# The gate's last two column blocks as a group of seven products, and a tile of the third normed block moved to another pool

## The chip, the cores and the metric

One core of a Trainium2 chip runs the whole program as one launch. The metric is the time of an execution on the device in microseconds, as the median of several runs. TensorE does the matrix products, VectorE and ScalarE the elementwise work, GpSimd (POOL) and SyncE (SP) mainly issue transfers.

## The reference

A decoder block on 256 tokens of width 2048, in float32: a half-step SwiGLU feed-forward, a mixer (gated DeltaNet and stick-breaking attention) between one input and one output projection, a second half-step feed-forward, then a gated embedding and a last norm. Only the end is touched by the change:

```python
h = h + 0.5 * swiglu(rms_norm(h, ffn2_norm), ffn2_w_gu, ffn2_w_down)
gate = jax.nn.sigmoid(rms_norm(h, ple_norm) @ ple_w_gate)   # 2048 x 2048
h = h + gate * (p @ ple_w_proj)                              # p: 256 x 256
return rms_norm(h, final_norm)
```

## The kernel before

**Products in three passes.** Each float32 operand is split into a high part (a cast to fp32r, on ScalarE) and a low part (the rest, on VectorE), and a product is three matmuls: high x high, high x low, low x high. Columns of weights come in blocks of 512, the contraction in steps of 256 ("pairs" of 128). A pair of weights is one transfer of 512 KB into `raw` (4 buffers), a cast `whi` and a subtraction `wlo` (`weight_pair`, 3 buffers each), and 12 matmuls: 2 halves of the pair x 2 tiles of 128 tokens x 3 passes.

**Groups of seven products.** A `Group` takes two column blocks and both token tiles, and does the first `ns` pairs of the contraction by a scheme of seven products for eight (`product`, `halved`, `all_sums`): each product is one token tile, 3 x `ns` matmuls, on sums of quarters of the weights (`R`, four tiles) and sums of the left sides (`Sh`, `Sl`, made by `halves`). The four results are in four PSUM banks `c11, c21, c12, c22`. ScalarE copies a first product from one bank to another (L349), or copies `c21` to `part` (L352) for VectorE to subtract (L354). Two of the sums of quarters are done by VectorE (L309), two by a transfer that accumulates, issued on POOL (L316). What is left of the contraction are plain pairs that add to the same banks. A group's seven products run between the plain pairs of the group before it.

**The order.** `plan` writes a list `order` of weight loads for the whole kernel; `next_weights` walks it and keeps two pairs and one sum split ahead of use. Side work (norms, transposes, left sides) is in generators, in four `Lanes`, each advanced one step after every plain pair. The program is written in this order and a scheduler fixes each engine's instruction order from it; the keyword `keep_in_program_order` pins a few.

**The end of the kernel.** The last group of the second feed-forward is the down projection of columns 1024 to 2047. Between its plain pairs run the products of "behind", the group of the gate's blocks 0 and 1 with `NS_BEHIND = 2`. `norm_block` prepares the normed, transposed, split `nT` per block of 512 columns of h. Blocks 0 to 2 go by VectorE transposes of 32 x 32 (`tb`), a store to DRAM on SP and four loads back into one tile `tT`, in the pool "ffn", then four scalings each on ScalarE (L162) and VectorE (L163). The last block goes by TensorE transposes. Block 2's seven steps reach into the plain pairs of "behind". Then the pool "ffn" ends and the pool "fin" begins, in the same memory: `fg` (the last norm's gain, 1 MB), `ph`/`pl` (p, split), `hf` (h times that gain, 2 x 2048 columns).

In "fin": the 12 plain pairs of "behind", sorted by twos over its two blocks; after each block's last pair the embedding product `embed` (one pair of `w_pp`, 12 matmuls) and `gated` (sigmoid on ScalarE, two operations on VectorE, `sumsq` on ScalarE, the product with `fg` on VectorE). Block 2 follows with 8 plain pairs for both token tiles. For block 3 all 8 weight pairs stay in memory; token tile 0 is one column range of 512, token tile 1 two of 256, so that its last `gated` is short. After each token tile come `rstd`, four scalings and four stores of the output.

Of the kernel before, what the change touches and what calls it, by code (L numbers as in the profile page):

```python
# [10 lines left out]
F32 = mybir.dt.float32  # L11
F32R = mybir.dt.float32r
AF = mybir.ActivationFunctionType
# [3 lines left out]
P = 128  # L17
# [12 lines left out]
NS = 4  # L30
# [7 lines left out]
W_IN_ORDER = (2, 0, 4, 3, 1, 5, 8, 10, 12, 9, 11, 13, 6, 7)  # L38

NS_BEHIND = 2  # L40

PLAIN = {"1": 2, "2": 1}
EPS = 1e-6
# [4 lines left out]
def block_kernel(ctx, tc, a, out):  # L48
# [69 lines left out]
    def products(ps_t, t, xs, ws, n):  # L118

        for g, (whi, wlo) in enumerate(ws):  # L120
            for j in range(2):
                k = 2 * g + j
                xh, xl = xs(k)
                c = slice(t * P, (t + 1) * P)
                nc.tensor.matmul(ps_t, xh[:, c], whi[:, j, n], start=k == 0, stop=False)
                nc.tensor.matmul(ps_t, xh[:, c], wlo[:, j, n], start=False, stop=False)
                nc.tensor.matmul(ps_t, xl[:, c], whi[:, j, n], start=False, stop=k == 2 * len(ws) - 1)
# [100 lines left out]
    def block(j):  # L228
        return slice(j * NB, (j + 1) * NB)
# [19 lines left out]
    class Group:  # L249
# [8 lines left out]
        def __init__(self, kind, part, src, quarters, ns, bank, nb=0):  # L258
            self.kind, self.part, self.src, self.ns, self.nb, self.bank = kind, part, src, ns, nb, bank
            self.quarters, self.raw, self.first = quarters, {}, False  # L260
            self.seven = SEVEN_DOWN if kind == "dn" and part and nb == 0 else SEVEN
# [94 lines left out]
    def plan(n):  # L356
# [22 lines left out]
        if n == "2":  # L379
            src = [sources("w_behind", b) for b in range(2)]  # L380
            groups.append(Group("behind", len(PARTS), [x[0] for x in src], [x[1] for x in src], NS_BEHIND,
                                len(groups) % 2))
        if n == "1":

            groups[0].plain.sort(key=lambda x: x[1])
        made, carried = [], []
        for i, group in enumerate(groups):
            group.follower = follower = groups[i + 1] if i + 1 < len(groups) else None
            after = groups[i + 2] if i + 2 < len(groups) else None
            n_plain = len(group.plain)  # L390
            at, loads, carried = [], {0: carried}, []
            if follower is not None and follower.ns:
                first = 8 if not group.ns else 4 if follower.kind == "behind" else \
                    1 if group.kind == follower.kind or group.part and follower.kind == "dn" else 2
                at = [min(first + j, n_plain - 1) for j in range(7)]
                if not group.ns:
                    follower.first = n

                    loads.setdefault(max(at[0] - 5, 0), []).extend(follower.loads())
                if after is not None and after.ns:  # L400
# [5 lines left out]
            for j, (b, g) in enumerate(group.plain):  # L406
                todo.append(("plain", (b, g)))
                order.append(("pair", group.src[b][g]))
                if group.kind == "behind" and g == KD // 2 - 1:
                    order.append(("pair", a["w_pp"][b]))  # L410
                for x in range(7):
                    if at and at[x] == j:
# [10 lines left out]
    order += [("pair", a["w_pg"][2][g]) for g in range(KD // 2)] + [("pair", a["w_pp"][2])]  # L423
    order.append(("pair", a["w_pp"][3]))

    def left_sides(kind, his, los):

# [51 lines left out]
    def ffn(n, nT, r, scale, next_norm, stat):  # L479
        xs = picker(*nT)  # L480
        late = callable(r)
        with tc.tile_pool(name="ffn", bufs=1) as fp:
# [71 lines left out]
            for group, todo in ffn_plan[n]:  # L554
# [17 lines left out]
                for kind, one in todo:  # L572
# [28 lines left out]
                    if dn:  # L601
# [89 lines left out]


    with tc.tile_pool(name="fin", bufs=1) as fp:
        fg = fp.tile([P, D], F32, tag="fg", name="fg")
        nc.scalar.dma_start(out=fg, in_=a["final_norm"].broadcast_to([P, D]))
        ph = fp.tile([P, 2, T], F32R, tag="ph", name="ph")
# [9 lines left out]

        lanes.add(2, split_p())
        stat = new_stat()
        hf = fp.tile([P, 2, D], F32, tag="hf", name="hf")
        xs = picker(*nT)  # L710

        def gated(e, gt, c, t, col):
# [4 lines left out]
            nc.vector.tensor_tensor(out=s, in0=e, in1=s, op=ALU.mult)  # L717
            nc.vector.tensor_tensor(out=h[:, t, c], in0=h[:, t, c], in1=s, op=ALU.add)
# [9 lines left out]
        group, todo = ffn_plan["2"][-1]  # L728
        for _, (nb, g) in todo:
            whi, wlo = next_weights()  # L730
            for j in range(2):
                k = 2 * g + j
                xh, xl = xs(k)
                for t in range(2):
                    c = slice(t * P, (t + 1) * P)
                    gt, sp = group.banks[2 * nb + t], k == KD - 1
                    nc.tensor.matmul(gt, xh[:, c], whi[:, j, :], start=False, stop=False, skip_group_check=True)
                    nc.tensor.matmul(gt, xh[:, c], wlo[:, j, :], start=False, stop=False, skip_group_check=True)
                    nc.tensor.matmul(gt, xl[:, c], whi[:, j, :], start=False, stop=sp, skip_group_check=True)
            lanes.step()  # L740
            if g == KD // 2 - 1:
                e = embed(mm_ps)
                for t in range(2):
                    gated(e[t], group.banks[2 * nb + t], block(nb), t, nb)
        gt = [mm_ps("gt") for _ in range(2)]
        accumulate(gt, xs, KD)
        e = embed(mx_ps)
        for t in range(2):
            gated(e[t], gt[t], block(2), t, 2)

        e = embed(mx_ps)
        ws = [weight_pair(a["w_pg"][3][g], fp, KD // 2) for g in range(KD // 2)]
        for t in range(2):
            n = NB >> t
            for i in range(NB // n):
                gt = mm_ps("gt")[:, 0:n]
                products(gt, t, xs, ws, slice(i * n, (i + 1) * n))
                gated(e[t][:, i * n:(i + 1) * n], gt, slice(3 * NB + i * n, 3 * NB + (i + 1) * n), t, 3 + i)
            rt = rstd(stat, t)
            for j in range(4):  # L760
                c = slice(j * NB, (j + 1) * NB)

                if j == 0:
                    nc.scalar.activation(hf[:, t, c], hf[:, t, c], AF.Copy, scale=rt)
                else:
                    nc.vector.tensor_scalar(out=hf[:, t, c], in0=hf[:, t, c], scalar1=rt, scalar2=None, op0=ALU.mult)
                queue = nc.sync if j % 2 else nc.scalar
                queue.dma_start(out=out[t * P:(t + 1) * P, c], in_=hf[:, t, c])


class Later:
# [621 lines left out]
def _layout(i):  # L1393
# [28 lines left out]
    m["w_pg"] = _blocks(f["ple_w_gate"][0])  # L1422
# [20 lines left out]
```

## Time and profile before

| | |
|---|---|
| median of 3 runs | 1943.84 us (1942.93 to 1944.59) |
| the profiled execution | 1942.55 us, of which the span from first to last instruction is 1940.5 us |
| busy, share of the span | TensorE 99%, weight load 82%, VectorE 81%, ScalarE 60%, POOL 8% |
| moved by DMA | 477.14 MB, mean 246 GB/s |
| granted TensorE clock | 0.999 |

A profile row has the line of the program, the engine, the operation, `out<-in` with the program's tile names, the shape, a count, the busy time and the mean of one. In a timeline row the first two numbers are the start and the duration in us, and a bracket names the idle time before it and what ended it. A row of a wait is: who waited, for whom, us in total, times, longest. A row by window has the window, its length, then busy us and count of TensorE, weight load, VectorE, ScalarE and POOL, the granted clock, the DMA's share and GB/s. An engine name with q (SPq, ACTq) is that engine's queue issuing a transfer.

### The profile page before, as it was taken

How to read it: one execution, taken by the hardware profiler on the slowest of the kernel's cores; microseconds unless marked ns; L12 is line 12 of the kernel's file. 1: busy time of each engine (PE TensorE's matmuls, PEld its weight loads, DVE VectorE, ACT ScalarE, POOL GpSimd, SP SyncE). 2: the span in 40 equal slices, each digit the busy share in tenths (PEclk: the TensorE clock that was granted, in tenths of full speed). 3: DMA queues.
4: the chain of work that ended last, by engine and by line, in shares of the span. 5: the costliest groups of instructions: out<-in, count | busy, mean ns of one | idle time of the engine just before them, and what ended most of it. 6: DMA issues, size and time to landing. Idle time of an engine off the chain costs nothing.

```text
span 1940.5 us, 24108 instructions
## 1 busy us (share of the span) xinstructions
PE 1925.3 (99%) x8872; PEld 1591.1 (82%) x8872; DVE 1580.8 (81%) x1701; ACT 1169.9 (60%) x1356; POOL 148.7 (8%) x226
## 2 busy tenths in 40 slices
PE   9999999999999999999999999999999999999998
PEld 7888888888888888878788888888888888888887
DVE  7879878998789766797856679899889998888865
ACT  6656666666666557664555456566556665666654
POOL 0011110001001000010100000010000100001000
PEclk9999999999999999999999999999999999999999
DMA  8778888888988665556564776788888988889764
GB/s 309 268 237 283 251 290 284 275 274 248 286 274 263 215 220 172 176 168 213 166 209 157 244 280 233 227 282 289 247 270 289 295 261 263 267 263 291 231 214 148
DMA packets 143029, 477.14 MB, mean 246 GB/s; under 512 B 19520, under 2 KB 47168, under 8 KB 125632
## 3 DMA queue, kind: packets, MB, share of 16 engines
q1 hardware_dynamic: 106048, 297.97, 43.8%
q0 software_dynamic: 25920, 166.74, 31.1%
q10 hardware_dynamic: 10944, 10.91, 1.8%
q8 instruction: 69, 1.13, 0.2%
q14 instruction: 48, 0.39, 0.1%
HBM read 453.53 MB, written 22.02 MB: 245 GB/s over the span
## 4 chain that ended last, share of the span: by engine, by line
PE 93%; DVE 4%; DMA 1%; issue 1%; ACT 0%; POOL 0%; SPq 0%; POOLq 0%; DVEq 0%; ACTq 0%
PE d L594 5%; PE d L596 5%; PE d L595 5%; PE u L595 5%; PE u L596 5%; PE u L594 5%; PE g L345 5%; PE g L346 5%; PE g L344 5%; PE g L595 4%; PE g L596 4%; PE pj L113 4%; PE pj L114 4%; PE pj L115 4%; PE g L594 4%; PE d L344 3%
## 5 line engine op out<-in xcount | busy, mean ns | idle before, releaser
L78 ACT CAST whi<-raw 128x1024 fp32r<-128x1024 f32 (+1 forms) x481 | 503.7, 1050 | 388.6 <-PE pj L115 109.0
L79 DVE TENSOR_TENSOR wlo<-raw,whi 128x1024 fp32r<-128x1024 f32 (+1 forms) x481 | 582.3, 1217 | 157.5 <-ACT whi L78 154.6
L301 DVE TENSOR_TENSOR slo<-R,shi 128x2048 fp32r<-128x2048 f32 (+2 forms) x224 | 459.9, 2054 | 122.5 <-ACT shi L300 120.6
L300 ACT CAST shi<-R 128x2048 fp32r<-128x2048 f32 (+2 forms) x224 | 386.1, 1725 | 147.8 <-DVE R L309 72.0
L113 PE MATMUL pj<-whi,nTh 128*128 128x512 f32 x448 | 179.4, 401 | 0.0
L114 PE MATMUL pj<-wlo,nTh 128*128 128x512 f32 x448 | 175.2, 391 | 1.2 <-DVE wlo L79 1.2
L115 PE MATMUL pj<-whi,nTl 128*128 128x512 f32 x448 | 174.9, 390 | 0.0
L594 PE MATMUL d<-whi,hTh 128*128 128x512 f32 x416 | 162.0, 390 | 0.0
L595 PE MATMUL d<-wlo,hTh 128*128 128x512 f32 x416 | 161.6, 389 | 0.0
L596 PE MATMUL d<-whi,hTl 128*128 128x512 f32 x416 | 160.6, 389 | 0.0
L595 PE MATMUL g<-wlo,nTh 128*128 128x512 f32 x400 | 156.2, 390 | 0.3 <-DVE wlo L79 0.2
L594 PE MATMUL g<-whi,nTh 128*128 128x512 f32 x400 | 155.2, 390 | 0.8 <-ACT nTh L162 0.6
L595 PE MATMUL u<-wlo,nTh 128*128 128x512 f32 x400 | 155.7, 389 | 0.2 <-DVE wlo L79 0.2
L596 PE MATMUL g<-whi,nTl 128*128 128x512 f32 x400 | 155.9, 390 | 0.0
L596 PE MATMUL u<-whi,nTl 128*128 128x512 f32 x400 | 155.6, 389 | 0.0
L594 PE MATMUL u<-whi,nTh 128*128 128x512 f32 x400 | 154.3, 389 | 0.0
L309 DVE TENSOR_TENSOR R<-R 128x2048 f32<-128x2048 f32 (+2 forms) x68 | 140.0, 2058 | 0.2
L114 PEld LDWEIGHTS pj<-wlo,nTh 128*128 128x128 f32 x448 | 84.2, 188 | 19.0 <-DVE wlo L79 2.8
L115 PEld LDWEIGHTS pj<-whi,nTl 128*128 128x128 f32 x448 | 84.1, 188 | 17.5
L113 PEld LDWEIGHTS pj<-whi,nTh 128*128 128x128 f32 x448 | 84.2, 188 | 16.7
L594 PEld LDWEIGHTS d<-whi,hTh 128*128 128x128 f32 x416 | 78.1, 188 | 17.5 <-ACT hTh L530 1.6
L596 PEld LDWEIGHTS d<-whi,hTl 128*128 128x128 f32 x416 | 78.1, 188 | 16.5
(346 smaller groups left out, 3488.9 us busy)
## 6 DMA issues: line engine op xcount, KB each, us to landing
raw<-in_w_gu SPq DMA_DIRECT2D x199, 512.0 KB, 5.9
raw<-in_w_in SPq DMA_DIRECT2D x112, 512.0 KB, 3.6
R<-in_w_gu2q POOLq DMA_DIRECT2D x54, 1024.0 KB, 8.4
raw<-in_w_down SPq DMA_DIRECT2D x104, 512.0 KB, 6.5
R<-in_w_gu1q POOLq DMA_DIRECT2D x48, 1024.0 KB, 8.7
raw<-in_w_out SPq DMA_DIRECT2D x32, 512.0 KB, 4.3
tT<-scr SPq DMA_DIRECT2D x22, 512.0 KB, 4.8
scr<-tb ACTq DMA_DIRECT2D x64, 128.0 KB, 5.4
```

Of the source, the lines that this page charges most:

```text
L78: nc.scalar.copy(hi[:, j, :], raw[:, j, :])
L79: nc.vector.tensor_tensor(out=lo[:, j, :], in0=raw[:, j, :], in1=hi[:, j, :], op=ALU.subtract)
L113: nc.tensor.matmul(outs[t], xh[:, c], whi[:, j, :], start=st, stop=False)
L114: nc.tensor.matmul(outs[t], xh[:, c], wlo[:, j, :], start=False, stop=False)
L115: nc.tensor.matmul(outs[t], xl[:, c], whi[:, j, :], start=False, stop=sp)
L300: keep(nc.scalar.copy(hi, w))
L301: nc.vector.tensor_tensor(out=lo, in0=w, in1=hi, op=ALU.subtract)
L309: keep(nc.vector.tensor_tensor(out=self.raw[x], in0=self.raw[x], in1=self.raw[y], op=ALU.add))
L344: nc.tensor.matmul(out, xh, whi[:, g, :], start=st, stop=False, skip_group_check=True)
L594: nc.tensor.matmul(out, xh[:, c], whi[:, j, :], start=st, stop=False, skip_group_check=True)
L595: nc.tensor.matmul(out, xh[:, c], wlo[:, j, :], start=False, stop=False, skip_group_check=True)
L596: nc.tensor.matmul(out, xl[:, c], whi[:, j, :], start=False, stop=sp, skip_group_check=True)
```

## The change

- A new group "fin" takes the gate's blocks 2 and 3 with `NS = 4` pairs by seven products, in the order `SEVEN_DOWN`. Its weights come as quarters (`w_fin`), its four `R` loads are issued on POOL at the start of the pool "fin", its left sides are made by `halves` in lane 1.
- Five of its products run between plain pairs of "behind" (after pairs 5, 6, 8, 9 and 11, `AT_FIN`), two between its own first plain pairs. The embeddings of blocks 0 and 1 are made together after pair 4 (`E_AT`) and copied to memory (`eb`) by ScalarE, since "fin" needs those PSUM banks.
- Block 2 keeps 4 plain pairs, block 3 keeps 4 per token tile; three of those weights come from the common buffers and one from the pool "fin". For token tile 1, the second half of `c22` is copied to another bank (`rest`) and both 256-wide halves add to what is there.
- The product with `fg` is written over `h` for blocks 0 to 2; `hf` keeps only block 3.
- For the third normed block (`nb == 2`) of the second feed-forward, the tile `tT` of the pool "ffn" is replaced by two tiles of the common `nat` tiles, one per token half: eight loads instead of four, and eight scalings of 128 columns on each engine instead of four of 256.

```diff
+E_AT = 4
+AT_FIN = 5, 6, 8, 9, 11
...
-        yield from transposed(lambda t: h[:, t, block(j)], tT)
+        tT = yield from transposed(lambda t: h[:, t, block(j)], tT)
         for kk in range(4):
+            if isinstance(tT, list):
+                for t in range(2):
+                    split_scaled(*(n[j][:, kk, t * P:(t + 1) * P].rearrange("p (q y) -> p q y", q=4) for n in (hi, lo)),
+                                 tT[t][:, :, 32 * kk:32 * kk + 32], gains[:, which, 4 * j + kk:4 * j + kk + 1])
+                if kk == 1:
+                    yield
+                continue
...
+            src = [sources("w_fin", b) for b in range(2)]
+            groups.append(Group("fin", len(PARTS), [x[0] for x in src], [x[1] for x in src], NS, len(groups) % 2))
...
-                at = [min(first + j, n_plain - 1) for j in range(7)]
+                at = AT_FIN if follower.kind == "fin" else [min(first + j, n_plain - 1) for j in range(7)]
...
-                if group.kind == "behind" and g == KD // 2 - 1:
-                    order.append(("pair", a["w_pp"][b]))
+                if group.kind == "behind" and j == E_AT:
+                    order.extend(("pair", a["w_pp"][x]) for x in range(2))
...
+                if group.kind == "fin" and j < 2:
+                    todo.append(("seventh", 5 + j))
+                    order.append(("sum", group))
+                    if j:
+                        order.append(("pair", a["w_pp"][2]))
...
-                            norm_block(nxt, next_norm, nb, lambda: fp.tile([P, 2, 4, P], F32, tag="tT", name="tT"),
+                            norm_block(nxt, next_norm, nb, lambda nb=nb: None if group.follower and nb == 2 else
+                                       fp.tile([P, 2, 4, P], F32, tag="tT", name="tT"),
...
+        (behind, todo), (last, todo_last) = ffn_plan["2"][-2:]
+        for _, load in last.loads():
+            last.queue = nc.gpsimd
+            load()
+        lanes.add(1, halves("fin", *nT, NS))
...
-            nc.vector.tensor_tensor(out=hf[:, t, c], in0=h[:, t, c], in1=fg[:, c], op=ALU.mult)
+            dst = h[:, t, c] if c.start < 3 * NB else hf[:, t, c.start - 3 * NB:c.stop - 3 * NB]
+            nc.vector.tensor_tensor(out=dst, in0=h[:, t, c], in1=fg[:, c], op=ALU.mult)
...
+            if step == E_AT:
+                for _ in range(2):
+                    e = embed(mm_ps)
+                    ebs.append([fp.tile([P, NB], F32, tag="eb", name="eb", bufs=4) for _ in range(2)])
+                    for t in range(2):
+                        nc.scalar.copy(ebs[-1][t], e[t])
...
+        c11, c21, c12, c22 = last.banks
+        for kind, one in todo_last:
+            if kind == "seventh":
+                last.product(last.seven[one])
+                if one == 6:
+                    e = embed(mx_ps)
+                continue
+            whi, wlo = next_weights()
+            for t in range(2):
+                plain(last.banks[t], t, whi, wlo, one[1])
...
+        rest = mm_ps("rest")[:, 0:half]
+        nc.scalar.copy(rest, c22[:, half:NB])
+        ws = [next_weights() for _ in range(KD // 2 - NS - 1)] + [weight_pair(a["w_fin"][1][KD // 2 - NS - 1], fp, 1)]
         for t in range(2):
...
+            for i, (gt, n) in enumerate(((c22[:, 0:half], slice(0, half)), (rest, slice(half, NB)))
+                                        if t else ((c12, slice(0, NB)),)):
+                for g, (whi, wlo) in enumerate(ws):
+                    plain(gt, t, whi, wlo, NS + g, n)
```

More of the change, by code (lines that the diff above doesn't have):

```diff
@@ L116, in accumulate @@
             lanes.step()
[L118 to L127, printed above, removed]
     zero = act.tile([P, NB], F32, tag="junk", name="zero", bufs=1)
@@ L260, in __init__ @@
             self.quarters, self.raw, self.first = quarters, {}, False
-            self.seven = SEVEN_DOWN if kind == "dn" and part and nb == 0 else SEVEN
+            self.seven = SEVEN_DOWN if kind == "dn" and part and nb == 0 or kind == "fin" else SEVEN
             self.last = part == len(PARTS) - 1
@@ L399, in plan @@
                     loads.setdefault(max(at[0] - 5, 0), []).extend(follower.loads())
-                if after is not None and after.ns:
+                if after is not None and after.ns and after.kind != "fin":
                     *three, last = after.loads(follower)
@@ L406, in plan @@
             for j, (b, g) in enumerate(group.plain):
+                if group.kind == "fin" and b:
+                    break
                 todo.append(("plain", (b, g)))
                 order.append(("pair", group.src[b][g]))
-                if group.kind == "behind" and g == KD // 2 - 1:
-                    order.append(("pair", a["w_pp"][b]))
+                if group.kind == "behind" and j == E_AT:
+                    order.extend(("pair", a["w_pp"][x]) for x in range(2))
                 for x in range(7):
-                    if at and at[x] == j:
+                    if x < len(at) and at[x] == j:
                         todo.append(("seventh", x))
                         order.append(("sum", follower))
+                if group.kind == "fin" and j < 2:
[3 more added lines that the diff above has]
+                        order.append(("pair", a["w_pp"][2]))
                 order.extend(loads.get(j, []))
@@ L422, in block_kernel @@
     ffn_plan["2"] = plan("2")
-    order += [("pair", a["w_pg"][2][g]) for g in range(KD // 2)] + [("pair", a["w_pp"][2])]
     order.append(("pair", a["w_pp"][3]))
+    order += [("pair", a["w_fin"][1][g]) for g in range(KD // 2 - NS - 1)]
     def left_sides(kind, his, los):
@@ L708, in block_kernel @@
         stat = new_stat()
-        hf = fp.tile([P, 2, D], F32, tag="hf", name="hf")
+        hf = fp.tile([P, 2, NB], F32, tag="hf", name="hf")
         xs = picker(*nT)
@@ L725, in embed @@
             return e
-        group, todo = ffn_plan["2"][-1]
-        for _, (nb, g) in todo:
-            whi, wlo = next_weights()
-            for j in range(2):
-                k = 2 * g + j
-                xh, xl = xs(k)
-                for t in range(2):
[L735 to L739, printed above, removed]
-            lanes.step()
[L741 to L744, printed above, removed]
@@ L745, in block_kernel, with plain @@
-        gt = [mm_ps("gt") for _ in range(2)]
-        accumulate(gt, xs, KD)
+        def plain(out, t, whi, wlo, g, n=slice(0, NB)):
+            c = slice(t * P, (t + 1) * P)
+            for j in range(2):
+                xh, xl = xs(2 * g + j)
+                sp = 2 * g + j == KD - 1
+                nc.tensor.matmul(out, xh[:, c], whi[:, j, n], start=False, stop=False, skip_group_check=True)
+                nc.tensor.matmul(out, xh[:, c], wlo[:, j, n], start=False, stop=False, skip_group_check=True)
+                nc.tensor.matmul(out, xl[:, c], whi[:, j, n], start=False, stop=sp, skip_group_check=True)
@@ new lines, in block_kernel @@
+        step, ebs = 0, []
+        for kind, one in todo:
+            if kind == "seventh":
+                last.product(last.seven[one])
+                continue
+            nb, g = one
+            whi, wlo = next_weights()
+            for t in range(2):
+                plain(behind.banks[2 * nb + t], t, whi, wlo, g)
+            lanes.step()
+            if step == E_AT:
[4 more added lines that the diff above has]
+                        nc.scalar.copy(ebs[-1][t], e[t])
+            step += 1
+            if g == KD // 2 - 1:
+                for t in range(2):
+                    gated(ebs[nb][t], behind.banks[2 * nb + t], block(nb), t, nb)
@@ L747, in block_kernel @@
+        c11, c21, c12, c22 = last.banks
+        for kind, one in todo_last:
+            if kind == "seventh":
+                last.product(last.seven[one])
+                if one == 6:
+                    e = embed(mx_ps)
+                continue
+            whi, wlo = next_weights()
+            for t in range(2):
+                plain(last.banks[t], t, whi, wlo, one[1])
+            lanes.step()
+        for t in range(2):
+            gated(e[t], last.banks[t], block(2), t, 2)
         e = embed(mx_ps)
+        half = NB // 2
@@ L748, in block_kernel @@
+        rest = mm_ps("rest")[:, 0:half]
+        nc.scalar.copy(rest, c22[:, half:NB])
+        ws = [next_weights() for _ in range(KD // 2 - NS - 1)] + [weight_pair(a["w_fin"][1][KD // 2 - NS - 1], fp, 1)]
         for t in range(2):
[L749 to L758, printed above, removed]
+            for i, (gt, n) in enumerate(((c22[:, 0:half], slice(0, half)), (rest, slice(half, NB)))
+                                        if t else ((c12, slice(0, NB)),)):
+                for g, (whi, wlo) in enumerate(ws):
+                    plain(gt, t, whi, wlo, NS + g, n)
+                gated(e[t][:, n], gt, slice(3 * NB + n.start, 3 * NB + n.stop), t, 3 + i)
@@ L1421, in _layout @@
     m["eye32"] = np.eye(32, dtype=np.float32).reshape(4, 256)
-    m["w_pg"] = _blocks(f["ple_w_gate"][0])
+    _parted(m, "w_fin", _blocks(f["ple_w_gate"][0])[2:4], NS)
     m["w_pp"] = np.ascontiguousarray(_blocks(f["ple_w_proj"][0])[:, 0])
```

8 lines of the change are left out of this document (5 added, 3 removed).

## The prediction

> **What bounds the kernel now.** I read the page first, then who waited for whom on TensorE, then the timeline of TensorE, VectorE, ScalarE and the queues from 1836 us on, which is all that the change touches, and last the stages by window.
>
> ```profile
> span 1940.5 us, 24108 instructions
> PE 1925.3 (99%) x8872; PEld 1591.1 (82%) x8872; DVE 1580.8 (81%) x1701; ACT 1169.9 (60%) x1356; POOL 148.7 (8%) x226
> PE pj L114 <- DVE wlo L79: 1.2, 3, 0.5
> 1843.50:1895.20 51.70, 51.70 (x229) 42.79 (x229) 32.92 (x42) 28.36 (x38) 0.71 (x1) 1.00 0.66 217
> ```
>
> TensorE is busy for all but 15 us, and its largest wait on anyone sums to 1.2 us. The last row is the stage from the first plain pair of "behind" over 51.7 us: TensorE has no gap in it at full clock, VectorE works 32.92 us, the DMA moves 217 GB/s. So the time is the number of matmuls times their step, plus whatever wait a change adds. A matmul's busy time overlaps the next one's; the step is read from starts:
>
> ```profile
> 1843.55 0.39 PE L737 MATMUL g<-whi,nTh 128*128 128x512 f32 x1
> 1854.43 0.39 PE L737 MATMUL g<-whi,nTh 128*128 128x512 f32 x1
> ...
> 1908.86 0.39 PE L125 MATMUL gt<-whi,nTh 128*128 128x512 f32 x1
> 1919.51 0.39 PE L127 MATMUL gt<-whi,nTl 128*128 128x512 f32 x1
> 1919.74 0.28 PE L125 MATMUL gt<-whi,nTh 128*128 128x256 f32 x1
> 1931.01 0.28 PE L126 MATMUL gt<-wlo,nTh 128*128 128x256 f32 x1
> ```
>
> The rows 1908.86 and 1919.51 are the 1st and 48th of 48: 10.65 / 47 = 0.2266 us for 512 columns. The last two are the 1st and 95th of 96: 11.27 / 94 = 0.1199 us for 256. The first two are the start of behind's plain pairs and of the fifth, 4 pairs of 12 matmuls later: 10.88 / 48 = 0.2267 again. A pair is 2.72 us; I call this a place. Each lost microsecond on TensorE is a microsecond of the kernel.
>
> **The matmuls, term one.** Blocks 2 and 3 of the gate cost before: 96 of 512 (block 2), 48 of 512 (block 3, first token tile), 96 of 256 (second tile). After: 7 products of 4 pairs, 12 matmuls each, 84; block 2's plain rest 4 x 12 = 48; block 3's rest 24 at 512 and 48 at 256. That is 156 of 512 and 48 of 256: +12 x 0.2266 - 48 x 0.1199 = 2.72 - 5.76 = **-3.04 us**. The four embeddings and behind's own matmuls keep their number. The gain is thus 0.16%, below the 0.2% that I take as what a measurement can tell from no change. The Trainium skill (TensorE: Matmul & The Clock Gate, Back-to-back issue gap) gives a warm gap of N/2.4 + 2.5 ns, 216 and 109 ns; an estimate by that page would be 2.59 - 5.24 = -2.65 us. The trace's steps are 5 and 10% longer, and the trace decides.
>
> **VectorE in that stage, term two.** In the 51.7 us (19 places: 12 pairs, 2 embeddings, the first 5 products) the work after is made of these rows.
>
> ```profile
> 1910.75 4.63 DVE L79 TENSOR_TENSOR wlo<-raw,whi 128x1024 fp32r<-128x1024 f32 x4
> 1189.25 4.49 DVE L301 TENSOR_TENSOR slo<-R,shi 128x2048 fp32r<-128x2048 f32 x2 [1.78 <-ACT shi L300]
> 1175.17 2.28 DVE L309 TENSOR_TENSOR R<-R 128x2048 f32<-128x2048 f32 x1
> 1163.13 1.80 DVE L456 TENSOR_TENSOR S<-S 128x256 f32<-128x256 f32 x4
> 1876.63 0.69 DVE L718 TENSOR_TENSOR h<-h,sg 128x512 f32<-128x512 f32 x1
> 1240.00:1280.00 40.00, 40.00 (x178) 33.11 (x178) 35.58 (x35) 24.41 (x27) 4.46 (x7) 1.00 0.74 242
> ```
>
> 14 pair splits at 4.63/4 = 16.2; 5 large splits at 4.49/2 = 11.2; two sums of quarters 4.6; the sides of fin, twice (1.16 + 1.80 + 1.16) = 8.2; the normed blocks some 4; the gates of block 0, six operations, 4.1; pl and two part subtractions 2.1. Sum 50.4 of 51.7 us, 97%, against 32.92 now. The most that a stretch shows with TensorE unbroken is the last row, 35.58 of 40, 89%. It can hold only if little waits on order. The part before the first product is the worst: 8 places, 21.8 us, in which 8 splits (9.3), the sides (8.2), the norms (4), pl and the first large split with its sum (4.6) come to 26.8. But the first product is due only at place 8 and the next at 10, and pairs are split two places ahead, so about 5 us of lag is absorbed. I take 0 on average here, with ends 0 and +4.9 us (50.4 / 0.89 = 56.6, less 51.7).
>
> **The third normed block, term three.** Before, it is ready just in time:
>
> ```profile
> 1843.32 0.39 PE L346 MATMUL g<-shi,nTl 128*128 128x512 f32 x1
> 1844.98 0.48 DVE L163 SCALAR_TENSOR_TENSOR nTl<-tr_n,gains,nTh 128x256 fp32r<-128x256 f32 x1
> 1844.48 2.53 SPq L187 DMA_DIRECT2D tT<-scr  x4
> DMA to landing us min/median/max: 3.9/4.4/5.0
> 1852.86 1.71 ACT L162 ACTIVATE nTh<-tT,gains 128x256 fp32r<-128x256 f32 x4
> 1854.14 1.67 DVE L163 SCALAR_TENSOR_TENSOR nTl<-tT,gains,nTh 128x256 fp32r<-128x256 f32 x4
> 1855.83 0.36 ACTq L695 DMA_DIRECT2D fg<-in_final_norm  x1
> 1845.16 0.71 POOL L243 TENSOR_TENSOR rstd<-rstd,mhalf 128x2 f32<-128x2 f32 x1 [18.35 <-DVE rstd L241]
> ```
>
> The fifth plain pair, at 1854.43, is the first to read this block; its third matmul (about 1854.9) needs the low part, whose first quarter is written by 1854.6. There is 0.3 us to spare. With a tile per token half, four transfers on SP become eight of half the size (0.63 us of issue each, if unchanged: to 1849.5), four scalings become eight on ScalarE and on VectorE (128 columns; at least half, at most all of the 0.43 us each), and the sides of fin stand ahead of them on VectorE. Landing at 4.4 us gives 1853.9, the first low part 0.43 + 0.42 later at 1854.8: no wait; at 5.0 us it is 0.6. VectorE, free at 1845.4 (the end of the row 1844.98), has to fit 3 splits (3.5) and the sides (8.2) first: 1857.1, 2.2 us late, if it takes them in that order. I take **+1.0 us** between 0 and 2.2, nearer to the first because splits wait for their ScalarE half in any order. An early landing would not gain: TensorE has no gap here.
>
> The pool: fg, first in the final stage's pool, is issued at 1855.83, just as the last read of this block's tile ends (1854.14 + 1.67), though its place in the program is before. With that tile out, the last readers of the pool are behind's products, the last at 1843.32; the four 1 MB loads then follow the rstd on POOL, from 1845.9.
>
> **The loads, term four.** What shows four such loads beside unbroken pairs is the start of the second feed-forward:
>
> ```profile
> 1151.08 2.06 SPq L281 DMA_DIRECT2D R<-in_w_gu2q  x4
> 1155.00:1160.00 5.00, 5.00 (x24) 4.14 (x23) 4.86 (x11) 3.35 (x4) 0.80 (x1) 1.00 1.00 421
> 1167.67 1.05 ACT L78 CAST whi<-raw 128x1024 fp32r<-128x1024 f32 x1 [0.17 <-DMA raw<-in_w_gu]
> 1169.89 1.90 ACT L300 CAST shi<-R 128x2048 fp32r<-128x2048 f32 x1
> DMA to landing us min/median/max: 3.5/8.0/13.1
> 1200.00:1240.00 40.00, 40.00 (x178) 33.14 (x177) 32.60 (x24) 22.34 (x21) 3.96 (x6) 1.00 0.93 290
> ```
>
> There the DMA reaches 421 GB/s, three pair splits wait for their data, and TensorE stays at 5.00 of 5. Here the first cast of R is due near place 6, 1860; even the longest landing of all R loads, 13.1 us, gives 1859.0. The stage then moves 11.2 MB (217 x 51.7) less 5 pairs (2.6) plus 4.2 of R and 2.1 of accumulation, 14.9 MB or 288 GB/s, which the last row carries. I take 0; ends 0 and +1. The eight half transfers share these engines with R, which is the weak point (rivals).
>
> **The end, term five.** The product before block 2's plain rest and the second token tile of that rest use one bank: ScalarE must copy it out in the 6 matmuls (1.36 us) between. Now such a copy starts at the end of its matmul and takes 0.59:
>
> ```profile
> 1750.54 0.59 ACT L352 COPY part<-d 128x512 f32<-128x512 f32 x1 [0.56 <-PE d L346]
> 1924.01 0.72 ACT L764 ACTIVATE hf<-hf,rstd 128x512 f32<-128x512 f32 x1 [1.11 <-POOL rstd L243]
> 1924.76 0.87 ACTq L768 DMA_DIRECT2D out_dram<-hf  x2
> 1931.45 0.47 ACT L716 ACTIVATE sg<-gt,rstd 128x256 f32<-128x256 f32 x1 [3.82 <-PE gt L127]
> ```
>
> Alone it fits; behind one large cast (1.90) it is 1.1 late: I take +0.2. The last tile's 256-wide part is now 5.76 us instead of 11.5, so its first gate, ready 2.9 us after the first tile, meets that tile's scaling and output issue on ScalarE, up to 1925.6 in today's row: 0 to +1.3, I take +0.3. In-place products with the final gain wait for the Square; only at the three early blocks, where VectorE has room afterwards: 0. The four copies of the early embeddings (0.59 each) lie on ScalarE, at 28.36 of 51.7: 0. The last four weight pairs are split in 8.2 us instead of 16: 0, ends 0 and +1.
>
> **Sum.** -3.04 + 0 + 1.0 + 0 + 0.2 + 0.3 = **-1.5 us**. The profiled execution took 1942.55 us (span 1940.5 and 2.05 around it), so 1941.0 for such a one; the median of runs is 1943.84, 1.29 above it, so I predict **1942.3 us**.
>
> **Rivals.** (a) Nothing waits: -3.0, 1940.8 us. For: TensorE waits for nobody today, and the start of the second feed-forward has the same load. Against: 0.3 us of slack at the fifth pair. (b) Slower: the third block's half transfers, issued to 1849.5 on SP, run among 4 MB of R from 1845.9 and land late; TensorE stands at the fifth pair. With the 0.5 of term five it breaks even at 2.5 us of wait (landing in 7.1 us) and is slower by 0.2% from 6.4 (11.0 us); at 13.1 us, the longest R landing, the low part is there at 1863.5, 8.6 late, +6.1: 1949.9 us. Against: those transfers are 64 KB, not 1 MB. The Trainium skill (DMA: Bandwidth & Descriptors, Issuing engines are not separate DMA queues) says that transfers of all issuing engines interleave on the same 16 engines, which speaks for this; the pair splits that wait beside R at 1167.67 agree. (c) VectorE binds: at 89% the stage lasts 4.9 us longer, with term five +2.4: 1946.2 us. (d) The pool does not free sooner: R starts at 1855.9, lands by 1863.9, cast and split (1.90 + 2.28) end at 1868.1, 2.8 us past place 8 (1865.3), with term five +0.3: 1944.1 us.
>
> **Chances.** Forecast 0.42 (loss 0.5 to 3 us: 1941.3 to 1943.8), a 0.25, b beyond 3 us of loss 0.13, c 0.15, d 0.05. Faster by over 0.2% (below 1940.0) needs more than term one gives: 0.05, out of a. Slower (above 1947.7): most of b and a little of c, 0.12. Same 0.83. The range takes in a, c and d and the near half of b: 1940.2 to 1947.7.
>
> **What would show it.** Term one: 84 products on fin's banks, 48 matmuls of 256. Term three: TensorE idle at the first pair that reads the third block, named after nTh or nTl. Term four: R loads on POOL near 1846, not 1856. Term two: VectorE over 45 us in the 51.7. Wrong would be a wait of TensorE above 3 us anywhere, or a tail from last matmul to end that differs from today's 9.4 us by over 1.5.

## The result, and the profile after

| | before | after |
|---|---|---|
| median of 6 runs each, taken together | 1943.70 us (1942.93 to 1944.86) | 1954.05 us (1953.44 to 1955.33) |
| profiled execution: time, span | 1942.55, 1940.5 us | 1953.75, 1952.0 us |

The ratio is 1.0053, with an interval of 1.0043 to 1.0064: slower by 10.35 us, where 1942.3 was predicted. The page of the changed kernel, and below it who TensorE waited for from 1835 us on:

```profile
span 1952.0 us, 24071 instructions
PE 1926.5 (99%) x8836; PEld 1590.6 (81%) x8836; DVE 1598.8 (82%) x1720; ACT 1179.4 (60%) x1370; POOL 152.6 (8%) x232
...
PE g L749 <- ACT nTh L154: 7.7, 1, 7.7
PE g L751 <- DVE nTl L155: 1.3, 1, 1.3
```

The page hides it: TensorE has 36 matmuls fewer, as planned (8872 to 8836), and is still "99%" busy, because 12 us in 1952 are 0.6%. The list of waits shows it at once: two waits, at one place, on the two halves of the third normed block. TensorE's timeline there, and the two ends of the stage:

```profile
1844.91 0.40 PE L749 MATMUL g<-whi,nTh 128*128 128x512 f32 x1
...
1863.61 0.80 PE L749 MATMUL g<-whi,nTh 128*128 128x512 f32 x1 [7.66 <-ACT nTh L154]
1864.21 0.63 PE L750 MATMUL g<-wlo,nTh 128*128 128x512 f32 x1
1864.63 0.63 PE L749 MATMUL g<-whi,nTh 128*128 128x512 f32 x1
...
1866.99 0.80 PE L751 MATMUL g<-whi,nTl 128*128 128x512 f32 x1 [1.30 <-DVE nTl L155]
1867.58 0.63 PE L749 MATMUL g<-whi,nTh 128*128 128x512 f32 x1
1868.01 0.63 PE L750 MATMUL g<-wlo,nTh 128*128 128x512 f32 x1
...
1870.50 0.39 PE L117 MATMUL e<-whi,ph 128*128 128x512 f32 x1
...
1941.64 0.28 PE L751 MATMUL rest<-whi,nTl 128*128 128x256 f32 x1
```

The first row is behind's first plain pair. The fifth is due four pairs later, at 1844.91 + 48 x 0.2267 = 1855.79, and starts at 1863.61. The embeddings, due 12 matmuls on at 1858.51, start at 1870.50: **12.0 us lost at the fifth pair**. Two waits are 9.0 of it. Between and after them the steps are about 0.43 us (1864.21 to 1864.63, 1867.58 to 1868.01) instead of 0.2267. The stages by window say why (the third number from the end is the granted clock):

```profile
1844.00:1856.00 12.00, 11.96 (x54) 9.56 (x52) 10.41 (x17) 5.17 (x10) 3.04 (x5) 1.00 0.89 335
1856.00:1866.00 10.00, 2.08 (x4) 1.16 (x4) 0.89 (x1) 2.84 (x8) 0.00 (x0) 0.71 0.98 367
1866.00:1868.00 2.00, 1.01 (x2) 0.84 (x3) 2.00 (x7) 2.00 (x3) 0.00 (x0) 0.50 0.39 113
1868.00:1870.00 2.00, 2.00 (x6) 1.62 (x5) 1.68 (x4) 2.00 (x3) 0.00 (x0) 0.50 0.45 170
1870.00:1872.00 2.00, 2.00 (x9) 1.61 (x9) 2.00 (x4) 1.49 (x3) 0.00 (x0) 0.90 0.30 41
1870.50:1941.50 71.00, 71.00 (x335) 59.63 (x334) 57.28 (x60) 43.39 (x56) 1.92 (x3) 1.00 0.48 134
```

In the ten us of the stand the DMA is 98% busy while VectorE works 0.89 us and ScalarE 2.84: everybody waits for transfers. Then TensorE runs at half its clock for the 12 matmuls of that pair: 12 steps about 0.2 us too long, some 2.5 us. From 1870.50 to the end it is never idle.

The sum closes. From first plain pair to last matmul: 96.73 us, before 87.58 (1843.55 to 1931.13), +9.15 = -3.04 (the matmuls) + 11.99 + 0.2. From last matmul to end: 10.36, before 9.37, +0.99. Together 10.14 of the 10.35. (The first plain pair itself starts between 1843.3 and 1845.7 us in the profiles of this case, so only distances from it are compared.)

What the half transfers did, by the tile and by the queues. The first two rows are the tile's, the next are timeline rows:

```profile
L177 SPq DMA_DIRECT2D tT<-scr x8: 302/454/737, 1844.5 to 1848.3; - x8
...
DMA to landing us min/median/max: 2.0/9.6/15.3
...
1845.10 0.36 ACTq L710 DMA_DIRECT2D fg<-in_final_norm  x1
...
1845.59 0.56 POOL L280 DMA_DIRECT2D R<-in_w_finq  x1 [17.42 <-DVE nTl L155]
...
1847.93 1.63 POOL L280 DMA_DIRECT2D R<-in_w_finq  x3
...
1863.16 0.99 ACT L154 ACTIVATE nTh<-tT,gains 128x128 fp32r<-128x128 f32 x3 [10.88 <-DMA tT<-scr]
```

Eight transfers of 64 KB, issued by 1848.8, landed after up to 15.3 us, where before this block's four of twice the size took 4.1 at most. Beside them 1 MB of fg and 4 MB of R were set off between 1845.1 and 1849.6. ScalarE stood 10.88 us for them. The second wait, 1.3 us for the low half, is one of order: VectorE's first low part stands behind a pair's split and a step of fin's left sides, and the cast that this split needs stands on ScalarE behind three scalings.

```profile
1865.11 1.23 DVE L83 TENSOR_TENSOR wlo<-raw,whi 128x1024 fp32r<-128x1024 f32 x1 [10.26 <-ACT whi L82]
1866.26 0.42 DVE L464 TENSOR_TENSOR S<-S 128x256 f32<-128x256 f32 x1
1866.59 0.34 DVE L155 SCALAR_TENSOR_TENSOR nTl<-tT,gains,nTh 128x128 fp32r<-128x128 f32 x1
```

### The profile page after: what moved, and what is told of

It is laid out like the page before. It is cut to its first block, busy times and chain, and to the rows that moved or that the text cites. A ratio compares the mean times of both kernels' runs of the same rounds, so it can differ in the third digit from the quotient of the medians.

```text
span 1952.0 us, 24071 instructions
## 1 busy us (share of the span) xinstructions
PE 1926.5 (99%) x8836; PEld 1590.6 (81%) x8836; DVE 1598.8 (82%) x1720; ACT 1179.4 (60%) x1370; POOL 152.6 (8%) x232
## 4 chain that ended last, share of the span: by engine, by line
PE 88%; DVE 6%; DMA 3%; issue 2%; ACT 1%; POOL 0%; SPq 0%; POOLq 0%; DVEq 0%; ACTq 0%
PE d L602 5%; PE d L604 5%; PE d L603 5%; PE g L344 5%; PE g L343 5%; PE g L345 5%; PE u L603 4%; PE u L604 4%; PE u L602 4%; PE pj L117 4%; PE pj L118 4%; PE pj L119 4%; PE g L603 4%; PE g L604 4%; PE g L602 4%; PE d L343 3%
## 5 line engine op out<-in xcount | busy, mean ns | idle before, releaser
L82 ACT CAST whi<-raw 128x1024 fp32r<-128x1024 f32 (+1 forms) x473 | 495.0, 1050 | 375.5 <-PE pj L119 106.2
L83 DVE TENSOR_TENSOR wlo<-raw,whi 128x1024 fp32r<-128x1024 f32 (+1 forms) x473 | 572.1, 1215 | 154.1 <-ACT whi L82 151.3
L300 DVE TENSOR_TENSOR slo<-R,shi 128x2048 fp32r<-128x2048 f32 (+2 forms) x231 | 475.6, 2060 | 127.0 <-ACT shi L299 125.0
L299 ACT CAST shi<-R 128x2048 fp32r<-128x2048 f32 (+2 forms) x231 | 399.5, 1731 | 153.6 <-DVE R L308 75.7
L308 DVE TENSOR_TENSOR R<-R 128x2048 f32<-128x2048 f32 (+2 forms) x70 | 144.4, 2063 | 0.2
L344 PE MATMUL g<-slo,nTh 128*128 128x512 f32 x246 | 96.1, 390 | 0.0
L345 PE MATMUL g<-shi,nTl 128*128 128x512 f32 x246 | 95.9, 390 | 0.0
```

The source lines that it names most:

```text
L82: nc.scalar.copy(hi[:, j, :], raw[:, j, :])
L83: nc.vector.tensor_tensor(out=lo[:, j, :], in0=raw[:, j, :], in1=hi[:, j, :], op=ALU.subtract)
L299: keep(nc.scalar.copy(hi, w))
L300: nc.vector.tensor_tensor(out=lo, in0=w, in1=hi, op=ALU.subtract)
L344: nc.tensor.matmul(out, xh, wlo[:, g, :], start=False, stop=False, skip_group_check=True)
L345: nc.tensor.matmul(out, xl, whi[:, g, :], start=False, stop=sp, skip_group_check=True)
```

## The experiments

Twelve kernels. "Lost" is the sum of what TensorE's steps took over 0.2267 and 0.12 us, from 1838 us on. It is read from one profiled execution, which lies up to 1.6 us from the median of its kernel (r_on_sp 1942.67 us, fg_late 1946.81), so it accounts for the median no closer than that. The edits are shown abridged.

**The eight half transfers by themselves** (norm_alone): the kernel before, with only its third normed block in two tiles.

```diff
+ tT = None for nb == 2 of the second feed-forward   # two shared tiles, eight loads, eight scalings
```

> The kernel before with one part of the change alone: the third normed block goes to two common tiles (eight half transfers, eight scalings of 128 columns); the gate is left as it was, so no R loads stand beside it, and only fg (1 MB) starts earlier. Sharing theory (the half transfers were late because 4 MB of R ran beside them): they land in 4 to 7 us instead of up to 15.3, TensorE waits less than 1.5 us at the fifth pair, time 1943 to 1946 us. Rival (eight half transfers are late by themselves, through their number, their issue or their tiles): TensorE waits 6 to 9 us at the fifth pair, time 1951 to 1956 us. Second rival (VectorE's order, the left sides ahead of the low parts): no left sides here, so no wait, and it is told from the first by the next run.

Measured: 1943.03 us, ratio 1.0000 (0.9991 to 1.0009). No wait of TensorE, 0.39 us lost. The transfers' row:

```profile
DMA to landing us min/median/max: 2.2/4.6/5.6
```

The halves and their doubled scalings cost nothing by themselves, though fg's 1 MB runs beside them here too. The left sides of fin are not in this kernel, so VectorE's order is not tested by it. What makes the transfers late is what else the change puts there.

**R behind the half transfers** (r_behind_tT): every load of R waits, by a small add on POOL, until both tiles have landed.

```diff
+ nc.gpsimd.tensor_tensor(out=raw[:, 0, 0:1], in0=landed[0][0][...], in1=landed[0][1][...], op=ALU.add)
  self.queue.dma_start(out=raw, in_=self.quarters[b][j])      # R, on POOL
```

> The changed kernel, but each R load on POOL first waits for the two landed tiles of the third normed block (a POOL addition of one column of them into the R tile, about 0.6 us each), so no byte of R moves beside the half transfers; fg still does. Sharing theory: last landing in 4 to 8 us instead of 15.3, TensorE waits 0 to 2 us at the fifth pair and keeps its full clock, R starts near 1853 and is in time or up to 2 us late for the first product: 1941 to 1945 us. Rival (eight by themselves): still a wait of 6 to 9 us, 1951 to 1955 us. VectorE's order: the wait for the low part stays at 1 us or more while the wait for the high part goes: 1943 to 1946 us.

**R on SP's queue** (r_on_sp): the four loads are issued by SP, in program order behind the eight.

```diff
- last.queue = nc.gpsimd; load()
+ if step == 1: load()     # on SP, kept behind tT
```

> The changed kernel with the four R loads on SP, issued behind the eight half transfers on the same queue (one 512 KB pair of w_pp stands among these) instead of on POOL beside them. Sharing theory: a transfer ahead in the same queue isn't passed by what follows it, so the half transfers land within 8 us, TensorE waits 0 to 2 us at the fifth pair; the pairs that follow R in the queue wait for 4 MB, about 10 us, which the two pairs ahead mostly cover: 1941 to 1945 us. If the 16 engines are shared by amount and not by queue, the landing stays above 10 us and the time above 1949 us.

Measured: 1945.88 us (ratio 1.0013, 1.0004 to 1.0022) and 1944.20 (1.0006, 0.9997 to 1.0015). Transfers and waits, first of r_behind_tT, then of r_on_sp:

```profile
DMA to landing us min/median/max: 1.9/4.7/5.6
...
PE g L753 <- ACT whi L82: 1.9, 1, 1.9
PE g L754 <- DVE wlo L83: 0.8, 1, 0.8
```

```profile
raw<-in_w_behind SPq DMA_DIRECT2D x4, 512.0 KB, 13.1
...
tT<-scr SPq DMA_DIRECT2D x8, 64.0 KB, 4.8
...
PE g L345 <- ACT g L350: 0.7, 1, 0.7
```

In both the wait at the fifth pair is gone, and 7.5 and 9.2 of the 10.35 us come back. The burst of 4 MB then makes other transfers late: issued at 1856.1 it meets the weights of the next pairs, and on SP the weights queue behind it (13.1 us to land). 5.9 and 3.0 us are still lost. The 1.9 us of r_behind_tT are a matter of order as well: that pair's weights had landed by 1863.5, but on ScalarE their cast, at 1865.55, stands behind the cast of R's first load. Its time lies 0.9 us above the range expected for it.

**The third-block part undone** (tT_in_pool): the change with that tile back in the pool "ffn".

```diff
- lambda nb=nb: None if group.follower and nb == 2 else fp.tile(..., tag="tT")
+ lambda: fp.tile(..., tag="tT")
```

> The changed kernel with the last part undone: the third normed block's tile is again one tile of the pool ffn, four transfers, and the pool frees only when it is read. Sharing theory: R starts near 1857 instead of 1846, the four transfers land in 4.4 us, no wait at the fifth pair; the first large cast waits for R, TensorE waits 2 to 5 us ahead of the first product: 1943 to 1947 us, so the pool part costs more than it gives. If the pool part were needed as meant: TensorE stands 8 us or more at the first product, 1950 us or above.

Measured: 1947.19 us, ratio 1.0021 (1.0012 to 1.0030). R's row and TensorE's waits:

```profile
L280 POOL DMA_DIRECT2D R<-in_w_finq x4: 535/543/602, 1857.3 to 1858.9; - x4
...
PE e L119 <- DVE pl L719: 2.3, 1, 2.3
PE g L344 <- DVE slo L300: 1.4, 1, 1.4
```

The pool then frees later, and R starts at 1857.3 instead of 1845.59, 11.7 us later. The embeddings wait 2.3 us for `pl`, the low part of p, which lies in the same memory, the first product waits 1.4 us for its weights, and with slow steps after the stand 6.7 us are lost. So the move does free the pool sooner, and it made the kernel 6 us slower all the same (10.35 above the kernel before, against 4.2 here), since what it sets free starts beside the half transfers.

**fg later** (fg_late): fg's 1 MB is loaded after the early embeddings; R stays beside tT.

```diff
- nc.scalar.dma_start(out=fg, in_=a["final_norm"].broadcast_to([P, D]))
+ # the same, after the copies of the embeddings
```

> The changed kernel with fg (1 MB) loaded only after the early embeddings, so that 4 MB instead of 5 MB run beside the half transfers; R stays on POOL. Sharing theory: the last landing falls with what shares the engines, from 15.3 to about 12 to 14 us; TensorE waits 5 to 7 us at the fifth pair: 1950 to 1953 us. If the queue of R alone decides (a share by queue that fg doesn't touch) the landing stays at 15 and the time at 1953.5 to 1954.5 us.

Measured: 1945.19 us, ratio 1.0009 (1.0001 to 1.0018), a miss for the expectation. Landing, the one wait, and R's issue on POOL:

```profile
DMA to landing us min/median/max: 2.0/6.1/7.1
...
PE g L748 <- ACT nTh L154: 2.0, 1, 2.0
...
1846.40 0.56 POOL L280 DMA_DIRECT2D R<-in_w_finq  x1 [17.45 <-DVE nTl L155]
...
1850.39 1.63 POOL L280 DMA_DIRECT2D R<-in_w_finq  x3
```

Two things had changed for the transfers: fg was away, and R's last three loads came 5.3 us behind the first half transfer (1845.1), not 3.5 us as in the changed kernel. The next two were to tell them apart. A third had changed on ScalarE, and it makes the wait that is left: the last half transfer is there by 1854.6, but ScalarE's order now has the cast of R's first load and three more casts ahead of the block's scaling.

```profile
1853.64 1.91 ACT L299 CAST shi<-R 128x2048 fp32r<-128x2048 f32 x1 [3.94 <-DMA R<-in_w_finq]
...
1858.29 1.27 ACT L154 ACTIVATE nTh<-tT,gains 128x128 fp32r<-128x128 f32 x4
```

**Three of R's loads later** (r_three_later): fg and the first of R stay as in the changed kernel; the other three wait until the first of the two tiles has landed.

```diff
+ nc.gpsimd.tensor_tensor(out=raw[:, 0, 0:1], in0=landed[0][0][...], ...)   # before loads 2 to 4 of R
```

> The changed kernel, but the last three of R's four 1 MB loads wait, by a one-column add on POOL, until the first tT tile (the first four 64 KB transfers) has landed; fg stays early on ACT's queue. It separates two readings of the run in which fg was loaded late: there tT landed in 7.1 us at most, but R's last three loads were also issued 5.3 us behind the first tT transfer, where the changed kernel issued them 3.5 us behind it. If R's spacing was what counted, tT lands in at most 8 us here, TensorE waits at most 2 us at the fifth pair and the time is 1944 to 1946. If fg as a third queue was what counted, fg and the first MB of R alone hold tT up, tT's last landing stays at 10 us or more, and with a wait of 4 us or more at the fifth pair the time is 1948 or more.

**fg on POOL's queue** (fg_on_pool): fg is issued just ahead of R.

```diff
- nc.scalar.dma_start(out=fg, ...)
+ nc.gpsimd.dma_start(out=fg, ...)      # then R's four
```

> The changed kernel, but fg is loaded on POOL's queue just ahead of R's four loads, so that the same 5 MB stand beside tT in one other queue in place of two. If the number of queues that move packets beside SP's is what makes the half transfers late, tT lands in 6 to 8 us and the time is 1944 to 1946.5. If the bytes beside it count, however they are queued, tT lands in 13 us or more at the last and the time is 1951 or more. R's last load is issued and lands about 3 us later than in the changed kernel either way, which costs nothing before the first of the seven products.

Measured: r_three_later 1943.75 us, ratio 1.0002 (0.9993 to 1.0011). The tile, and the stage, TensorE's second window unbroken:

```profile
L177 SPq DMA_DIRECT2D tT<-scr x8: 303/438/578, 1844.3 to 1847.8; - x8
...
DMA to landing us min/median/max: 2.1/7.2/8.1
...
1855.23 1.66 POOL L285 DMA_DIRECT2D R<-in_w_finq  x3
...
1844.60:1896.30 51.70, 49.85 (x219) 40.64 (x218) 46.73 (x53) 37.38 (x48) 5.33 (x10) 1.00 0.89 288
1862.00:1930.00 68.00, 68.00 (x314) 56.78 (x314) 55.34 (x54) 42.01 (x53) 1.75 (x2) 1.00 0.54 174
```

This is the answer: three loads issued at 1855.2 instead of 1847.9, and 10.2 of 10.35 us come back, with fg where the change has it. A wait of 1.6 us for nTl is left of the 9.0; the first low part starts at 1858.12, again behind a pair's split and a step of the sides on VectorE. The run of fg on POOL (1945.77, ratio 1.0009, 0.9999 to 1.0018) tells nothing on the number of queues: there POOL's rstd came first in its order, fg and R were issued from 1849.4 on, and tT had landed, in 2.1 us. It shows the transfers alone, and again waits for weights (0.9 and 1.8 us).

**TensorE kept busy through the wait** (filled_wait): 34 matmuls into a spare bank before the fifth pair.

```diff
+ if step == 4: 34 x nc.tensor.matmul(busy, nT[0][0][:, 0, 0:P], nT[0][0][:, 0:2, :])
```

> The changed kernel with 34 matmuls of 512 columns on loaded data into a free bank put ahead of the fifth plain pair, where TensorE stands 7.7 us (34 x 0.2266 = 7.7 us; their result is used nowhere). The half transfers land as late as before. Theory that the stand costs twice, once as a wait and once as a halved clock (0.50 granted, steps of 0.43 us for some 12 matmuls afterwards): the steps after the fill stay at 0.227 us, and the time falls by 2 to 3 us to 1951 to 1952.5 us, although TensorE does 7.7 us more work. Rival (the slow steps come from the late operands and not from the clock): no change or up to 1 us slower, 1953.5 to 1955 us.

Measured: 1959.85 us, ratio 1.0082 (1.0069 to 1.0095), outside both expectations. The waits, and VectorE's timeline at the last of them:

```profile
PE g L750 <- DVE wlo L83: 3.3, 1, 3.3
PE g L751 <- DVE nTl L155: 2.9, 2, 2.6
...
1871.98 4.49 DVE L300 TENSOR_TENSOR slo<-R,shi 128x2048 fp32r<-128x2048 f32 x2
1876.38 2.29 DVE L308 TENSOR_TENSOR R<-R 128x2048 f32<-128x2048 f32 x1
1878.59 3.49 DVE L83 TENSOR_TENSOR wlo<-raw,whi 128x1024 fp32r<-128x1024 f32 x3
```

The filling took the place of the first wait, but the second (2.6 us) stayed and the clock halved after it anyway. With the added matmuls the scheduler also set 6.8 us of R's work ahead of the pairs' splits on VectorE, which made a wait of 3.3 us that the changed kernel doesn't have. So this run doesn't isolate the price of the halved clock.

**Ways to a faster one.** r_on_sp_fg_late is r_on_sp with fg late; r_on_sp_fg_late_tail moves also the first row block's scaling from ScalarE to VectorE.

```diff
+ r_on_sp_fg_late: R on SP behind tT, fg after the embeddings
+ r_on_sp_fg_late_tail: the same, and  if j == 0 and t: nc.scalar.activation(...)  else: nc.vector.tensor_scalar(...)
```

> Both: R on SP behind the half transfers, and fg late. Nothing shares the engines with the half transfers. Sharing theory: landing 4 to 5 us, no wait at the fifth pair, and the pairs that follow R land about 2.5 us earlier than with fg beside them, so that the 2.6 us that TensorE still loses with R on SP alone shrink to 0.3 to 1.5: 1941.0 to 1942.8 us, against 1943.0 for the kernel before, first gain. If the loss behind R on SP comes from ScalarE and VectorE being full (VectorE theory), it stays at 2 to 3 us: 1943 to 1944.5 us.

> As the run before it, and the first token tile's first output scaling goes to VectorE, so that the last half block's sigmoid isn't queued on ScalarE behind a scaling that waits for the rstd on POOL. The stretch from the last matmul to the end, 10.2 to 10.4 us in the changed kernels against 9.4 before, falls to 9.4 to 9.7: 1940.3 to 1942.2 us. If the stretch is set by POOL and the transfers, it stays at 10.2 or above and the time is that of the run before.

Measured: 1944.24 us (1.0004, 0.9995 to 1.0013) and 1944.96 (1.0007, 0.9998 to 1.0016). Both miss the gain that was expected, though the half transfers land in 3.0 us at most, and both lose 3.2 us of TensorE to late weights and a late copy. The weights are late on ScalarE and not on the queue: in the first run the three pairs had landed by 1867.1, and their casts, from 1870.96, stand behind a cast of R. That speaks for the rival, by ScalarE's order rather than by its being full. In the second, TensorE's last result is read by ScalarE at once, but VectorE's scaling of the other rows stands ahead of its next step, and from last matmul to end it is still 10.65 us (1931.45 to 1942.1).

```diff
+ combined: {1: r_loads[:1], 2: r_loads[1:2], 3: r_loads[2:]}.get(step)  on SP, weights kept in order between them;
+           fg late; the first rows scaled after the last gate, all on ScalarE
+ three_later_fg_late: r_three_later with fg after the embeddings
```

> The changed kernel with what the runs so far point to: R's loads on SP's queue behind tT, spread so that one or two 512 KB weight loads go between them, fg loaded after the early embeddings, and the first row block's last scaling held behind the last gate, all of it on ACT, the second's all on VectorE. Theory (TensorE is lost only to late transfers and to the tail): the 3.2 us that TensorE lost with R on SP and fg late fall to about 1.5, the tail from the last matmul to the end falls from 10.2 to about 9.8, and the time is 1941.5 to 1943, 0.9988 to 0.9997 of before. Rival (the work that stands beside the first steps is short on VectorE and ScalarE, however the loads lie): TensorE still loses 3 us or more between 1843 and 1885 and the time is 1943.5 to 1945.

> The changed kernel with both repairs that helped, each done once already: R's last three loads wait until the first tT tile has landed, and fg's 1 MB is loaded after the early embeddings, so that only 1 MB of R stands beside tT. If the half transfers' lateness follows the bytes that stand beside them, tT's last landing falls from 8.1 us (2 MB beside it) to about 5 to 6, the 1.6 us that TensorE still waited at the fifth pair go, R's last three are issued about 3 us sooner, and the time is 1941.5 to 1943.2, at or a little below before. If it is the first MB of R on POOL's queue that counts, tT still lands at 7 to 8 us and the time stays at 1943.3 to 1944.5. The price that could eat the gain: R's three loads then meet the raw weights of the fifth to seventh pairs, and TensorE waits for whi or wlo there.

Measured: combined 1957.13 us (1.0071, 1.0059 to 1.0084), a plain miss:

```profile
PE g L752 <- ACT whi L85: 5.0, 1, 5.0
PE e L120 <- ACT whi L85: 1.7, 1, 1.7
```

With SP's order written out by hand, weights stood behind R on that queue and came up to 13.7 us after their issue; 13.7 us were lost. Its end took 12.5 us (1943.62 to 1956.1), with both row blocks' outputs leaving together. three_later_fg_late is 1944.02 us (1.0003, 0.9994 to 1.0012): tT landed in 6.1 us at most, as the bytes foretold, but TensorE lost 3.8 us, among them 1.1 for nTh, whose scaling ScalarE starts at 1855.01, behind the cast of R's first load and three others, and 1.0 for wlo. No version beats the kernel before.

## Why the prediction was wrong

- **Term three is the step that failed.** It took a landing of 4.4 to 5.0 us from the row of before (which holds twelve transfers of three blocks; this block's four took 3.9 to 4.1) and priced only what the change does to the tile itself: issue, scalings, VectorE's order, +1.0. Its own ends reach to 2.2. The transfers and scalings by themselves cost nothing (norm_alone). VectorE's order, which the term did name, is the 1.3 us of the second wait. The first wait, 7.7 us, comes because the same edit frees the pool, as the prediction's next paragraph has it, and so sets R off 11.7 us sooner (against tT_in_pool), onto the engines that carry the tile: the slowest landing took 15.3 us. Both waits sum to 9.0 us, where 1.0 was taken.
- **Rival (b) had the mechanism, at the place and on the operand that stopped TensorE**, and the prediction gave it 0.13. Its "against", that the transfers are 64 KB and not 1 MB, was no protection: they landed in 15.3 us, later than the slowest R load (13.9). Its price, +6.1, was low mostly by one thing that wasn't in it, the halved clock after the stand (about 2.5 us). The stand itself was 9.0 us and not 8.6, the end cost 1.0 and not 0.5, and 0.5 more went in the first steps after each wait.
- **Term four used a mean.** 288 GB/s over 51.7 us is what r_three_later moves, with hardly a wait. But the 5 MB are issued in the first 5 us, and the rows show 335 and 367 GB/s at 89 and 98% for 22 us. R itself landed in time (8.6 to 13.9 us): the loads had no cost, what they delayed had. The second feed-forward's start, taken as the precedent, has no small transfer that is due within 5 us.
- **Term one was right**: 48 matmuls of 256 columns are left, and with the burst moved (r_three_later) the stretch from first plain pair to last matmul is 87.10 us against 87.58 before: -3.04, with the 2.6 us that TensorE lost there put on.
- **Term two's 0 was right, its 50.4 us somewhat high**: VectorE works 46.73 us of the 51.7 in r_three_later. In the changed kernel TensorE is unbroken for 71.00 us beside it. Rival (c), 4.9 us by VectorE's rate, is out; what VectorE cost was its order (1.3 us, and 1.6 in r_three_later). So is (d): R was issued at 1845.59, near the 1846 predicted.
- **Term five** took 0.2 for a late copy that did not occur and 0.3 for the last tile, which measured +0.99. The first rows' scaling stands ahead of the last gate on ScalarE:

```profile
1942.05 0.72 ACT L807 ACTIVATE h<-h,rstd 128x512 f32<-128x512 f32 x1 [0.33 <-POOL rstd L242]
...
1942.68 0.46 ACT L731 ACTIVATE sg<-rest,rstd 128x256 f32<-128x256 f32 x1
```

The gate was ready 0.3 us after the last matmul and starts 1.04 after it.

The sentence of the Trainium skill that the prediction leant on for (b) (DMA: Bandwidth & Descriptors, Issuing engines are not separate DMA queues) held: from 1843 to 1866 us the queues of POOL, SP and ACT took 47.1, 34.2 and 11.8% of the time of the same 16 engines.

What stays open is how the engines share out their time. The slowest landing of tT was 2.1 us with no other queue's load beside it (fg_on_pool), 5.6 and 6.1 with 1 MB, 8.1 with 2 MB, 7.1 with R alone and three of its loads 5.3 us behind, and 15.3 with 5 MB at once. The single landings of the changed kernel show a pattern: the third to the seventh half transfer land at 1851.46, 1854.40, 1857.23, 1860.00 and 1863.14 us, each 0.2 to 0.3 us behind one of the 1 MB loads (fg at 1851.20, R at 1854.20, 1857.04, 1859.82 and 1862.95), though R's last three were issued 1.2 to 1.5 us behind the half transfers that landed after them. So one half transfer got through per large load; whether the number of these loads or their bytes counts is not told apart, since all were of 1 MB. The Trainium skill (DMA: Bandwidth & Descriptors, Queues, rings and completion order) says that each engine takes turns between queues packet by packet, which would leave a queue of short rows the smaller share. In the changed kernel from 1843 to 1866 us R's queue moved 4.19 MB in 576 packets and SP's 2.68 MB in 1915, which fits, but no run here changed the row length. Nor was the price of the halved clock isolated: it is read from steps.

## What to carry to other kernels

When an edit frees memory or an engine sooner, ask which transfers that lets go, at what microsecond, and which small transfer with a near due time they will share the engines with: price that landing beside the burst, not as the old profile shows it alone. A mean rate over a stage says nothing about a burst in its first microseconds. A transfer that is needed late should be held until the urgent one is through, but only as far as the next urgent one. Where each engine's order is fixed ahead, see also what stands behind the first reader of a load that may be late: in several of these kernels (fg_late, r_behind_tT, r_on_sp_fg_late) a cast of R on ScalarE held up work whose data had landed.

## What the hardware showed that was not expected

- A stand of TensorE costs more than itself. After single stands of 1.97 us (fg_late) and 2.34 us (tT_in_pool) the granted clock fell to 0.50 in the next 2 us window; after 1.64 us (r_three_later) it stayed at 1.00. The rows of fg_late and of r_three_later just after their stands:

```profile
1860.00:1862.00 2.00, 2.00 (x5) 1.61 (x6) 2.00 (x3) 2.00 (x6) 0.00 (x0) 0.50 1.04 438
```

```profile
1860.00:1862.00 2.00, 1.79 (x8) 1.21 (x7) 1.67 (x2) 2.00 (x3) 0.00 (x0) 1.00 0.96 375
```

  The Trainium skill (TensorE: Matmul & The Clock Gate, Why this matters for your kernels) warns of gaps over about 3 us; here a single stand of 1.97 us was enough, and the measurement decides. How long a stand must be isn't settled: the clock also fell to 0.50 after 1.75 us with 0.93 us shortly ahead of it (fg_on_pool) and after 1.90 with 0.76 us shortly behind it (r_behind_tT).
- A 64 KB transfer can take longer than a 1 MB one issued after it: in the changed kernel the seventh half transfer took 15.3 us, the three 1 MB loads of R issued after it 9.1 to 13.9. With no other queue's load beside them the half transfers took 2.1 us at most.
